# An RWKV-7 / HGRN2 mixer on one core: the RWKV state scan on half tiles of TensorE, one projection moved, and new planner figures

## The chip, the core and the metric

The kernel runs on one NeuronCore of a Trainium2 chip. The metric is the device time of one execution in microseconds (us). Before the change its median over 3 runs is 1031.55 us (1031.42 to 1031.56). TensorE is called PE below (PEld is its weight load, which overlaps the products), VectorE DVE, ScalarE ACT, GpSimd POOL, SyncE SP.

## The reference, cut to what matters

One layer over 512 frames of width 2048, in float32. One input projection feeds two mixers: 16 RWKV-7 heads of 64 columns, and 8 HGRN2 heads of 128. The gated outputs are concatenated, projected back, added to the residual and normalised. The part that the change rewrites is the recurrence of an RWKV head over its 64x64 state S:

```python
def step(S, inp):
    r_t, w_t, k_t, v_t, a_t, b_t = inp
    sa = jnp.einsum('bhij,bhj->bhi', S, a_t)
    S = S * w_t[:, :, None, :] + sa[..., None] * b_t[:, :, None, :] + v_t[..., None] * k_t[:, :, None, :]
    return S, jnp.einsum('bhij,bhj->bhi', S, r_t)
```

The kernel evaluates it in 8 chunks of 64 frames. Within a chunk, 64x64 score matrices and one triangular inverse stand for the recurrence; only the 64x64 state goes from chunk to chunk, one step of the scan for each.

## The kernel before, in words

**The bulk.** Both projections are dense products with 128x128 stationary tiles and 512 moving columns. Each float32 operand is split into a high and a low part (`xh`, `xl`; `wh`, `wl`), and `three` (L485) issues three products for each pair of tiles. This takes 3948 products of that kind on PE, those of the small preparations in the same number format included. The weights come in by DMA into `wr`, ACT makes `wh` and DVE `wl`.

**The rest** is recorded by small helpers, so that its instructions have the helpers' lines: `mm` (L348) for float32 products, `act` (L361, L362) on ACT, `tt` (L371), `stt` (L380), `copy` (L413) on DVE. A float32 product is two instructions in the profile. Heads are treated in pairs (`p` = 0 to 7), and pairs in groups of two (`grp` = 0 to 3), so four heads at a time. For a group there are, in this order: scores (`rwkv_prep`, 64-row stationary tiles), the inversion (`rwkv_invert`, 32x32 tiles), `folded` (64x64 tiles), `rwkv_scan`, and `outputs` (128-row tiles of 64 columns).

**The scan before.** The states of the two heads of a pair lie as the two 64x64 blocks on the diagonal of a 128x128 tile `bd`, whose other blocks are zero. A step of the scan has two bursts on PE. The first (called the state burst below) multiplies the stationary `ar` with the old state: two products of 128x128x128, one for each pair, into `mix` banks. DVE subtracts the upper half from `zz`, ACT scales the old state into the other `bd`, and ACT or DVE copies the lower half into the output tile. The second (the update burst) multiplies `bk` with `zz`, again two whole products, and DVE adds the diagonal blocks to the state, with four `stt` of 64x64. There are 7 steps with a state burst and 7 with an update burst in each group, 56 bursts in all.

**What sets the order.** All instructions are put in order when the program is built. `Plan` holds a clock for each engine and adds a cost figure for every operation. It lets the dense products run through, and takes the next operation of a thread (a generator for a head, a group, an eviction) when its operands should be there by the figures. PE's products are of three modes: `main` (the dense ones), `whole` (float32, full tiles) and `narrow` (a stationary tile of fewer than 128 rows or columns). `TURNS` holds a figure for each change of mode (0.1 into narrow, 0.11 out of it). After a narrow burst no other begins for 1.5 by the plan's clock (`REST`), and a burst that is ready is held back for a moment so that another may join it (`HOLD`). `_order` lists the projections, one for each name and number: k, r, v, z, q, f, g and i.

Of the kernel before, what the change touches and what calls it, by code (L numbers as in the profile page):

```python
# [7 lines left out]
F32 = mybir.dt.float32  # L8
# [30 lines left out]
def _order():  # L39

    o = [("w", 0)]
    for g in range(NPAIR // 2):
        for p in (2 * g, 2 * g + 1):
            o += [("k", p), ("r", p), ("v", p)]
            if g:
                o.append(("z", p - 2))
        o += [("q", 2 * g), ("f", 2 * g), ("q", 2 * g + 1), ("f", 2 * g + 1)]
        if g % 2 == 0:
            o.append(("i", g // 2))
        o += [("g", 2 * g), ("g", 2 * g + 1)]  # L50
    return o + [("z", NPAIR - 2), ("z", NPAIR - 1)]


# [3 lines left out]
    return o + [(2, 14), (2, 15), (3, 13), (3, 14), (3, 15)]  # L57


SETS = {AF.Sigmoid: ("sigmoid",), AF.Tanh: ("exp", "sigmoid"), AF.Exp: ("exp", "ln"), AF.Ln: ("ln",)}  # L60


class Plan:
# [194 lines left out]
def mixer_kernel(ctx, tc, head, x_r, w_all, par, up, ln_wb, consts, hmask, out):  # L258
# [25 lines left out]
    def take(tag, shape=(P, T), dt=F32):  # L284

        if not plan.free(tag):
            raise RuntimeError(f"no room: {tag}")
        slot = min(plan.slots[tag])
        plan.slots[tag].remove(slot)
        if tag in PBUFS:  # L290
            t = ppool.tile(list(shape), dt, tag=tag, name=nm(tag), bufs=PBUFS[tag])
            plan.banks.add(t.tensor.name)
        else:
            t = st(tag, list(shape), dt)
        name = t.tensor.name
        plan.busy[name] = (slot[1], None)
        tags[name] = tag
        return t

    def drop(*tiles):  # L300
        for t in tiles:
            name = t.tensor.name
            plan.slots[tags.pop(name)].append((plan.used.get(name, plan.count), plan.busy[name][0]))
# [27 lines left out]
    def size(ap):  # L331
        n = 1
        for s in ap.shape[1:]:
            n *= s
        return n

    def mm(o, l, r, start=True, stop=True, cost=None, **kw):
        m, n = size(l), size(r)
        narrow = m < P or l.shape[0] < P
        if cost:  # L340
            pass
        elif r.dtype == F32R:
            cost = n / 2400 + 0.0145
        elif narrow:
            cost = 0.0135 + n * 0.0002 if m <= 32 else 0.06 if m <= 64 else 0.115
        else:
            cost = n / 600 + 0.005
        return Op([("pe", cost, lambda: pe.matmul(o, l, r, start=start, stop=stop, **kw))], [l, r], [o],  # L348
                  mode="narrow" if narrow else "main" if r.dtype == F32R else "whole")
# [4 lines left out]
    def moved(o, i):  # L354

        return 0.1 if o.shape[0] < P else 0.0

    def act_way(o, i, f, scale=1.0, bias=0.0):
        cost = 0.09 + size(o) * 0.00085 + moved(o, i) + (0.06 if isinstance(scale, bass.AP) else 0.0)
        if f == AF.Copy:  # L360
            return "act", cost, lambda: sc_e.activation(o, i, f, scale=scale)  # L361
        return "act", cost, lambda: sc_e.activation(o, i, f, scale=scale, bias=bias)  # L362
# [4 lines left out]
    def dve_op(reads, o, f, n=None, per=0.00104, base=0.07):  # L367
        return Op([("dve", base + (n or size(o)) * per, f)], reads, [o])

    def tt(o, a, b, f=ALU.mult):  # L370
        return dve_op([a, b], o, lambda: dve.tensor_tensor(o, a, b, f),  # L371
                      base=0.16 if o.shape[0] < P and size(o) == C and o.tensor.name in tags else 0.07)

    def ts(o, a, s1, s2, f1, f2=None):
        if f2 is None:
            return dve_op([a], o, lambda: dve.tensor_scalar(o, a, s1, None, f1), per=0.0008)
        return dve_op([a], o, lambda: dve.tensor_scalar(o, a, s1, s2, f1, f2), per=0.0008)

    def stt(o, a, s, b, f1, f2):
        return dve_op([a, b], o, lambda: dve.scalar_tensor_tensor(o, a, s, b, f1, f2), per=0.00113,  # L380
                      base=0.085 if o.shape[0] == P else 0.25 if size(o) == C else 0.165)

    def red(o, i):
        return dve_op([i], o, lambda: dve.tensor_reduce(o, i, AX.X, ALU.add), size(i))
# [2 lines left out]
        return dve_op([i], o, lambda: dve.copy_predicated(o, m, i))  # L387

    def dtr(o, i):
        return dve_op([i], o, lambda: dve.transpose(o, i), per=0.0019)  # L390

    def dve_tt_way(o, a, b, f=ALU.mult):
# [12 lines left out]
    def memset(o, v):  # L405
        return Op([("pool", 0.1 + size(o) * 0.00083, lambda: pool.memset(o, v))], [], [o])

    def copy(o, i, scale=1.0):

        if scale != 1.0:  # L410
            f = lambda: dve.tensor_scalar(o, i, scale, None, ALU.mult)
        else:
            f = lambda: dve.tensor_copy(o, i)  # L413
        return Op([act_way(o, i, AF.Copy, scale), ("dve", 0.075 + size(o) * 0.00105 + moved(o, i), f)], [i], [o])

    def blocks(t, n):

# [2 lines left out]
    def turned(dst, src, tmp, rows=4):  # L420

        far = dpool.tile([P, rows, size(tmp) // rows], F32, tag=nm("far"), name=nm("far"))
        yield dtr(tmp.rearrange("p b c j -> p c b j"), src)
        yield lambda: by_now(tmp)
        yield lambda: plan.clock["sp"] <= plan.clock["pe"] + 0.2
        send(far, tmp.rearrange("p b c j -> p b (c j)"))
        there = plan.busy[tmp.tensor.name] = (plan.clock["sp"] + 4.0, "dma")
        for b in range(rows):
            yield lambda: there[0] <= plan.clock["pe"] and plan.clock["sp"] <= plan.clock["pe"] + 0.2
            send(dst(b).rearrange("i a c j -> i a (c j)"), far[:, b].rearrange("(a i) x -> i a x", a=4))  # L430
        plan.ready[dst(0).tensor.name] = (plan.clock["sp"] + 4.0, "dma")

# [236 lines left out]
    def head_sums(f, g, hl):  # L669

        own = slice(0, 64)
        yield tt(f[own], f[own], g[own], ALU.add)
        yield act(hl[own], f[own], AF.Copy)
        yield tt(hl[64:128], f[own], hl[own].bitcast(F32), ALU.subtract)

    def rwkv_prep(S, p):
        if p == 0:
# [227 lines left out]
    def rwkv_scan(SS, sc):  # L905

        pcs, ars, bks, zzs, os = ([S[n] for S in SS] for n in ("pc", "ar", "bk", "zz", "o"))  # L910
        yield room(bd=4)
        bdss = [[take("bd", [P, P]) for _ in range(2)] for _ in SS]

        def block(ps, h):
            return ps[hc[h], h * 64 : h * 64 + 64]

        for bds, o in zip(bdss, os):
            for t in bds:
                yield memset(t, 0.0)
            yield memset(o[0:64, 0], 0.0)  # L920
        olds = [None] * 2
        for c in range(NCH):
            more = c < NCH - 1
            zs = [zz[:, :, c] for zz in zzs]
            news = [bds[c % 2] for bds in bdss]
            pxs = []
            if c > 0:
                yield landed(*olds)
                yield room(mix=2)
                for ar, old in zip(ars, olds):  # L930
                    pxs.append(take("mix"))
                    yield mm(pxs[-1][:, :P], ar[:, c], old)
                for px, z in zip(pxs, zs):
                    yield tt(z[0:64], z[0:64], px[0:64, :P].rearrange("p (a j) -> p a j", j=32), ALU.subtract)
                if more:
                    for new, old, pc in zip(news, olds, pcs):
                        yield act(new, old, AF.Copy, scale=pc[:, c : c + 1])
                for px, o in zip(pxs, os):
                    yield copy(o[64 * (c % 2) : 64 * (c % 2) + 64, c // 2], px[64:128, :P])
                    drop(px)  # L940
            if more:
                yield landed(*zzs)
                yield room(mix=2)
                pds = [take("mix") for _ in SS]
                for pd, bk, z in zip(pds, bks, zs):
                    yield mm(pd[:, :P], bk[:, c], z)
                for pd, new, pc in zip(pds, news, pcs):
                    for h in range(2):
                        yield stt(new[hc[h], hc[h]], block(pd, h), pc[hc[h], c : c + 1],
                                  new[hc[h], hc[h]], ALU.mult, ALU.add)  # L950
                    drop(pd)
                olds = news
        drop(*ars, *bks, *pcs, *bdss[0], *bdss[1])

# [795 lines left out]
```

## Time and profile before

| | |
|---|---|
| median of 3 runs | 1031.55 us |
| the profiled execution's own time | 1033.02 us |
| its span, from the first to the last instruction | 1031.2 us |
| what lies around the span | 1.8 us |
| PE, DVE, ACT, POOL busy | 1020.1, 789.9, 478.4, 42.6 us |
| mean granted clock of TensorE | 1.000 |

The profiled execution took 1.47 us longer than the median. "Busy" counts each instruction from its start to its end, so that products that overlap in the array count as one stretch. A row of the groups or of a tile reads: line, engine, operation, written tile<-read tiles, stationary rows*columns, (partitions)x(moving columns), count | busy us, mean ns | idle time before. A row of the timeline reads: start us, us, engine, line, operation, tiles, count of merged instructions.

### The profile page before, as it was taken

Reading aid. Unit: us, or ns where it says so; the run is one execution under the profiler, and the core shown is the slowest. Engines: PE = TensorE matmul, PEld = TensorE weight load, DVE = VectorE, ACT = ScalarE, POOL = GpSimd, SP = SyncE. Lnnn points to the kernel's source line nnn. Section 1 sums busy time; section 2 is a strip of 40 time slices with the busy share of each in tenths; the row PEclk is TensorE's granted clock in tenths of the full one; section 3 lists DMA queues with packets and bytes.
Section 4 is the critical chain, followed back from the end, with each engine's and each line's share of the span. In section 5 each row is a group of like instructions: output and inputs, shape, how many; then the busy total and the mean of one; then the engine's idle time right before and its main releaser. Section 6 shows DMA issues by size and latency. Waiting matters only on the chain.

```text
span 1031.2 us, 19527 instructions
## 1 busy us (share of the span) xinstructions
PE 1020.1 (99%) x7636; PEld 843.2 (82%) x7636; DVE 789.9 (77%) x1687; ACT 478.4 (46%) x898; POOL 42.6 (4%) x77
## 2 busy tenths in 40 slices
PE   9999999999999999999999999999999999999997
PEld 8888878888878888888887888887888888888885
DVE  7477997679779988698998758887998888526556
ACT  6457344545363356464534554636435544323321
POOL 0000001001000010020000100100001010000000
PEclk9999999999999999999999999999999999999999
DMA  9134442233635322345353243253432256435613
GB/s 337 53 104 127 138 125 88 78 103 113 183 105 157 122 73 81 92 138 183 105 152 105 82 114 118 92 172 111 147 106 81 63 175 226 149 117 172 200 55 133
DMA packets 58700, 130.82 MB, mean 127 GB/s; under 512 B 9840, under 2 KB 25712, under 8 KB 58480
## 3 DMA queue, kind: packets, MB, share of 16 engines
q1 hardware_dynamic: 58464, 129.37, 39.7%
q8 instruction: 60, 0.98, 0.4%
q14 instruction: 32, 0.26, 0.1%
q10 hardware_dynamic: 144, 0.20, 0.1%
HBM read 111.06 MB, written 18.48 MB: 126 GB/s over the span
## 4 chain that ended last, share of the span: by engine, by line
PE 94%; DMA 2%; DVE 2%; ACT 1%; issue 1%; SPq 0%; DVEq 0%; ACTq 0%
PE main L485 71%; PE mix L348 9%; PE mix L485 8%; PE main L1275 3%; PE main L348 2%; DMA q<-far 1%; DMA far<-q 1%; PE mix L1225 0%; DVE inv L380 0%; SPq L327 0%; DVE wl L371 0%; DVE big L371 0%; DVE q L413 0%; DVE big L390 0%; ACT wh L361 0%
## 5 line engine op out<-in xcount | busy, mean ns | idle before, releaser
L485 PE MATMUL main<-xh,wl 128*128 128x512 f32 x864 | 340.0, 393 | 0.0
L485 PE MATMUL main<-xh,wh 128*128 128x512 f32 x864 | 339.5, 393 | 0.0
L485 PE MATMUL main<-xl,wh 128*128 128x512 f32 x864 | 339.0, 392 | 0.0
L361 ACT ACTIVATE wh<-wr 128x512 fp32r<-128x512 f32 x299 | 185.7, 626 | 194.4 <-PE main L485 139.0
L371 DVE TENSOR_TENSOR wl<-wr,wh 128x512 fp32r<-128x512 f32 x299 | 203.6, 682 | 56.0 <-ACT wh L361 53.9
L485 PEld LDWEIGHTS main<-xh,wh 128*128 128x128 f32 x864 | 162.4, 188 | 33.1
L485 PEld LDWEIGHTS main<-xh,wl 128*128 128x128 f32 x864 | 162.3, 188 | 33.1
L485 PEld LDWEIGHTS main<-xl,wh 128*128 128x128 f32 x864 | 162.3, 188 | 33.0
L485 PE MATMUL main<-wh,xl 128*128 128x512 f32 (+1 forms) x262 | 102.4, 391 | 0.0
L485 PE MATMUL main<-wh,xh 128*128 128x512 f32 (+1 forms) x262 | 101.8, 389 | 0.5 <-ACT t L362 0.5
L485 PE MATMUL main<-wl,xh 128*128 128x512 f32 (+1 forms) x262 | 101.9, 389 | 0.0
L485 PEld LDWEIGHTS main<-wh,xh 128*128 128x128 f32 x262 | 49.2, 188 | 10.8 <-ACT t L362 1.0
L485 PEld LDWEIGHTS main<-wh,xl 128*128 128x128 f32 x262 | 49.2, 188 | 10.0
L485 PEld LDWEIGHTS main<-wl,xh 128*128 128x128 f32 x262 | 49.2, 188 | 9.9
L362 ACT ACTIVATE t<-main,om 128x512 f32<-128x512 f32 x33 | 22.3, 686 | 51.9 <-PE main L485 42.6
L380 DVE SCALAR_TENSOR_TENSOR bd<-mix,pc,bd 64x64 f32<-64x64 f32 x112 | 31.7, 283 | 11.6 <-PE mix L348 7.8
L371 DVE TENSOR_TENSOR inv<-inv,inv 64x30 f32<-64x30 f32 (+14 forms) x120 | 38.5, 321 | 2.7
L371 DVE TENSOR_TENSOR inv<-inv 64x30 f32<-64x30 f32 (+14 forms) x120 | 38.5, 321 | 2.5
L380 DVE SCALAR_TENSOR_TENSOR t<-main,pr,t 128x511 f32<-128x511 f32 x33 | 24.3, 745 | 19.6 <-ACT t L362 19.5
L361 ACT ACTIVATE t<-mix 64x128 f32<-64x128 f32 (+2 forms) x66 | 18.0, 276 | 44.3 <-DVE zz L371 23.5
L371 DVE TENSOR_TENSOR t<-t,tot 128x256 f32<-128x256 f32 x96 | 37.2, 418 | 0.2
L362 ACT ACTIVATE t<-main 128x512 f32<-128x512 f32 x32 | 18.6, 593 | 28.7 <-PE main L485 28.6
(228 smaller groups left out, 1408.1 us busy)
## 6 DMA issues: line engine op xcount, KB each, us to landing
wr<-w_all SPq DMA_DIRECT2D x156, 512.0 KB, 3.6
q<-head SPq DMA_DIRECT2D x15, 448.0 KB, 5.8
far<-ksq SPq DMA_DIRECT2D x22, 256.0 KB, 3.2
far<-q SPq DMA_DIRECT2D x8, 512.0 KB, 5.0
q<-far SPq DMA_DIRECT2D x32, 128.0 KB, 4.4
g<-x_r SPq DMA_DIRECT2D x16, 256.0 KB, 4.0
t<-far SPq DMA_DIRECT2D x56, 64.0 KB, 3.5
spill<-g SPq DMA_DIRECT2D x12, 256.0 KB, 2.8
```

Of the source, the lines that this page charges most:

```text
L348: return Op([("pe", cost, lambda: pe.matmul(o, l, r, start=start, stop=stop, **kw))], [l, r], [o], mode="narrow" if narrow else "main" if ...
L361: return "act", cost, lambda: sc_e.activation(o, i, f, scale=scale)
L362: return "act", cost, lambda: sc_e.activation(o, i, f, scale=scale, bias=bias)
L371: return dve_op([a, b], o, lambda: dve.tensor_tensor(o, a, b, f), base=0.16 if o.shape[0] < P and size(o) == C and o.tensor.name in tags e ...
L380: return dve_op([a, b], o, lambda: dve.scalar_tensor_tensor(o, a, s, b, f1, f2), per=0.00113, base=0.085 if o.shape[0] == P else 0.25 if s ...
L485: pe.matmul(ps, l, r, start=first and i == 0, stop=last and i == 2)
L1275: pe.matmul(pss[a], *ops, start=k == 0 and low == of == 0, stop=k == KT - 1 and low == 1)
```

## The change

1. The states of a pair's two heads are stacked in one tile `bd` of 128 rows and 64 columns (the first head in rows 0 to 63, the second in rows 64 to 127). The state burst becomes four products with 64 stationary rows and 128 columns, 64 moving columns each; the two heads of a pair go to two banks and lie on the two row halves of the array. The update burst becomes four products with 128 stationary rows and 64 columns, 64 moving columns; the two heads go to the two column halves, all in one bank. In the planner they are narrow, at 0.07 and 0.063 a product.
2. Round them: four subtractions and four copies of 64x64 where there were two each of 64x128; two `stt` of 128x64 in place of four of 64x64; the scaled copy is 128x64; half of the clearing of `bd` is left out.
3. `_order`: in the groups 0 and 2 the first of the two g projections (an HGRN gate) stands ahead of the i projection.
4. Figures of the planner: DVE costs that depend on where the operand lies (`banked`), other bases for `stt` and the DVE transpose, a landing time that grows with the size (`late`), and Exp without the `ln` table. The argument 0.15 in `head_sums` has no effect there, since the condition behind it in `tt` does not hold for a tile of 512 columns. None of these figures adds or removes an instruction.

```diff
-        if g % 2 == 0:
-            o.append(("i", g // 2))
-        o += [("g", 2 * g), ("g", 2 * g + 1)]
+        o.append(("g", 2 * g))
+        if g % 2 == 0:
+            o.append(("i", g // 2))
+        o.append(("g", 2 * g + 1))
...
-SETS = {AF.Sigmoid: ("sigmoid",), AF.Tanh: ("exp", "sigmoid"), AF.Exp: ("exp", "ln"), AF.Ln: ("ln",)}
+SETS = {AF.Sigmoid: ("sigmoid",), AF.Tanh: ("exp", "sigmoid"), AF.Exp: ("exp",), AF.Ln: ("ln",)}
...
+    def banked(ap):
+
+        return 0.00104 if ap.tensor.name in plan.banks else 0.00076
...
-                      base=0.085 if o.shape[0] == P else 0.25 if size(o) == C else 0.165)
+                      base=0.085 if o.shape[0] == P and size(o) > P else 0.12 if o.shape[0] == P
+                      else 0.21 if size(o) == C else 0.165)
...
+        late = 4.2 + max(0, size(tmp) - T) * 0.002
+        there = plan.busy[tmp.tensor.name] = (plan.clock["sp"] + late, "dma")
...
-        bdss = [[take("bd", [P, P]) for _ in range(2)] for _ in SS]
+        bdss = [[take("bd", [P, C]) for _ in range(2)] for _ in SS]
...
-                for ar, old in zip(ars, olds):
-                    pxs.append(take("mix"))
-                    yield mm(pxs[-1][:, :P], ar[:, c], old)
-                for px, z in zip(pxs, zs):
-                    yield tt(z[0:64], z[0:64], px[0:64, :P].rearrange("p (a j) -> p a j", j=32), ALU.subtract)
+                pxs = [take("mix") for h in range(2)]
+                for i, (ar, old) in enumerate(zip(ars, olds)):
+                    for h in range(2):
+                        yield mm(pxs[h][:, i * C : i * C + C], ar[hc[h], c], old[hc[h]], cost=0.07)
+                for i, z in enumerate(zzs):
+                    for h in range(2):
+                        zh = z[0:64, hb[h], c]
+                        yield tt(zh, zh, pxs[h][0:64, i * C : i * C + C].rearrange("p (a j) -> p a j", j=32),
+                                 ALU.subtract)
...
-                pds = [take("mix") for _ in SS]
-                for pd, bk, z in zip(pds, bks, zs):
-                    yield mm(pd[:, :P], bk[:, c], z)
-                for pd, new, pc in zip(pds, news, pcs):
-                    for h in range(2):
-                        yield stt(new[hc[h], hc[h]], block(pd, h), pc[hc[h], c : c + 1],
-                                  new[hc[h], hc[h]], ALU.mult, ALU.add)
-                    drop(pd)
+                pd = take("mix")
+                for i, (bk, z) in enumerate(zip(bks, zzs)):
+                    for h in range(2):
+                        yield mm(pd[hc[h], i * C : i * C + C], bk[:, c, hc[h]], z[:, hb[h], c], cost=0.063)
+                for i, (new, pc) in enumerate(zip(news, pcs)):
+                    yield stt(new, pd[:, i * C : i * C + C], pc[:, c : c + 1], new, ALU.mult, ALU.add)
+                drop(pd)
```

The first place in the order is PE at a state burst of the first group, before. `main` with `xh` and `xl` is the dense stream; `bd` is the state, `q` holds `ar`, `mix` is a bank.

```order
L485 MATMUL main_2182<-xh_70,wh_2128 128x512
L485 MATMUL main_2182<-xl_86,wh_2128 128x512
L348 MATMUL mix_2198<-bd_2144,q_449 128x128
L348 MATMUL mix_2207<-bd_2146,q_756 128x128
L485 MATMUL main_2182<-xh_70,wl_2129 128x512
L485 MATMUL main_2182<-xh_71,wh_2128 128x512
```

And a state burst of the same group in the changed program.

```order
L494 MATMUL main_2319<-xh_78,wh_2341 128x512
L494 MATMUL main_2319<-xl_94,wh_2341 128x512
L349 MATMUL mix_2425<-bd_2232,q_449 128x64
L349 MATMUL mix_2426<-bd_2232,q_449 128x64
L349 MATMUL mix_2425<-bd_2234,q_769 128x64
L349 MATMUL mix_2426<-bd_2234,q_769 128x64
L494 MATMUL main_2319<-xh_78,wl_2342 128x512
L494 MATMUL main_2319<-xh_79,wh_2341 128x512
```

Two products became four, and they still stand alone between dense products. Of the 28 state bursts of the program, 21 stand alone like this in the changed order, 6 next to whole products and one next to narrow ones; of the 28 update bursts 22 stand alone, 3 next to whole and 3 next to narrow products.

The second place is PE at the outputs of the first group, before (`zz` and `big` are the inputs of `outputs`).

```order
L485 MATMUL main_2506<-xh_83,wl_2559 128x512
L348 MATMUL mix_2620<-zz_1080,big_713 64x64 x16
L348 MATMUL mix_2621<-zz_1377,big_713 64x64 x16
L485 MATMUL main_2680<-xh_68,wh_2585 128x512
L485 MATMUL main_2680<-xl_84,wh_2585 128x512
```

And the same place in the changed program, where `q` with `q` are the scores of a later pair.

```order
L494 MATMUL main_2748<-xh_73,wh_2733 128x512
L349 MATMUL mix_2779<-zz_1044,big_719 64x64 x16
L349 MATMUL mix_2780<-zz_1351,big_719 64x64 x16
L349 MATMUL main_2825<-q_2323,q_2324 128x128
L349 MATMUL main_2826<-q_2323,q_2324 128x128
L349 MATMUL main_2825<-q_2323,q_2324 128x128
```

A narrow burst of scores has joined the outputs here, and again in the third group; 32x32 products of the inversion join 48-column ones twice instead of once. In all, PE has 102 bursts between dense products before and 100 after. The last group's outputs stand behind 3156 dense products before and behind 3189 after.

The third place is DVE in a step of the first group's scan, before (`wl` is the dense stream's share of DVE).

```order
L371 TENSOR_TENSOR zz_1080<-zz_1080,mix_2255 64x4x32
L371 TENSOR_TENSOR zz_1377<-zz_1377,mix_2265 64x4x32
L413 COPY t_951<-mix_2265 64x128
L380 SCALAR_TENSOR_TENSOR bd_2144<-mix_2280,pc_646,bd_2144 64x64 x2
L380 SCALAR_TENSOR_TENSOR bd_2146<-mix_2281,pc_903,bd_2146 64x64
L371 TENSOR_TENSOR wl_2296<-wr_2174,wh_2295 128x512
L380 SCALAR_TENSOR_TENSOR bd_2146<-mix_2281,pc_903,bd_2146 64x64
```

And in the changed program.

```order
L372 TENSOR_TENSOR zz_1044<-zz_1044,mix_2425 64x2x32
L372 TENSOR_TENSOR zz_1044<-zz_1044,mix_2426 64x2x32
L372 TENSOR_TENSOR zz_1351<-zz_1351,mix_2425 64x2x32
L372 TENSOR_TENSOR zz_1351<-zz_1351,mix_2426 64x2x32
L397 STREAM_TRANSPOSE ksq_2430<-t_967 128x4x4x32
L372 TENSOR_TENSOR wl_2470<-wr_2288,wh_2469 128x512
L385 SCALAR_TENSOR_TENSOR bd_2233<-mix_2467,pc_667,bd_2233 128x64
```

Four subtractions stand where two stood, and one `stt` for each pair where two stood. Over the program the counts on DVE go from 112 to 56 for the `stt` on `bd`, from 56 to 112 for the subtractions, and from 28 to 45 for the copies of `mix` into the output tile; on ACT those copies go from 28 to 67. The number of dense products (3948) is the same.

More of the change, by code (lines that the diff above doesn't have):

```diff
@@ L368, in dve_op, with tt @@
         return Op([("dve", base + (n or size(o)) * per, f)], reads, [o])
-    def tt(o, a, b, f=ALU.mult):
+    def tt(o, a, b, f=ALU.mult, base=None):
         return dve_op([a, b], o, lambda: dve.tensor_tensor(o, a, b, f),
-                      base=0.16 if o.shape[0] < P and size(o) == C and o.tensor.name in tags else 0.07)
+                      base=base or 0.16 if o.shape[0] < P and size(o) == C and o.tensor.name in tags else 0.07)
+    def banked(ap):
+        return 0.00104 if ap.tensor.name in plan.banks else 0.00076
     def ts(o, a, s1, s2, f1, f2=None):
         if f2 is None:
-            return dve_op([a], o, lambda: dve.tensor_scalar(o, a, s1, None, f1), per=0.0008)
-        return dve_op([a], o, lambda: dve.tensor_scalar(o, a, s1, s2, f1, f2), per=0.0008)
+            return dve_op([a], o, lambda: dve.tensor_scalar(o, a, s1, None, f1), per=banked(a))
+        return dve_op([a], o, lambda: dve.tensor_scalar(o, a, s1, s2, f1, f2), per=banked(a))
     def stt(o, a, s, b, f1, f2):
         return dve_op([a, b], o, lambda: dve.scalar_tensor_tensor(o, a, s, b, f1, f2), per=0.00113,
-                      base=0.085 if o.shape[0] == P else 0.25 if size(o) == C else 0.165)
+                      base=0.085 if o.shape[0] == P and size(o) > P else 0.12 if o.shape[0] == P
+                      else 0.21 if size(o) == C else 0.165)
     def red(o, i):
@@ L389, in dtr @@
     def dtr(o, i):
+        if i.shape[0] == P:
+            return dve_op([i], o, lambda: dve.transpose(o, i), per=0.0011, base=0.05)
         return dve_op([i], o, lambda: dve.transpose(o, i), per=0.0019)
@@ L413, in copy @@
             f = lambda: dve.tensor_copy(o, i)
-        return Op([act_way(o, i, AF.Copy, scale), ("dve", 0.075 + size(o) * 0.00105 + moved(o, i), f)], [i], [o])
+        return Op([act_way(o, i, AF.Copy, scale), ("dve", 0.07 + size(o) * banked(i) + moved(o, i), f)], [i], [o])
     def blocks(t, n):
@@ L426, in turned @@
         send(far, tmp.rearrange("p b c j -> p b (c j)"))
-        there = plan.busy[tmp.tensor.name] = (plan.clock["sp"] + 4.0, "dma")
+        late = 4.2 + max(0, size(tmp) - T) * 0.002
+        there = plan.busy[tmp.tensor.name] = (plan.clock["sp"] + late, "dma")
         for b in range(rows):
@@ L430, in turned @@
             send(dst(b).rearrange("i a c j -> i a (c j)"), far[:, b].rearrange("(a i) x -> i a x", a=4))
-        plan.ready[dst(0).tensor.name] = (plan.clock["sp"] + 4.0, "dma")
+        plan.ready[dst(0).tensor.name] = (plan.clock["sp"] + late, "dma")
     splits = plan.queue()
@@ L673, in head_sums @@
         yield act(hl[own], f[own], AF.Copy)
-        yield tt(hl[64:128], f[own], hl[own].bitcast(F32), ALU.subtract)
+        yield tt(hl[64:128], f[own], hl[own].bitcast(F32), ALU.subtract, 0.15)
     def rwkv_prep(S, p):
@@ L911, in rwkv_scan @@
         yield room(bd=4)
-        bdss = [[take("bd", [P, P]) for _ in range(2)] for _ in SS]
-        def block(ps, h):
-            return ps[hc[h], h * 64 : h * 64 + 64]
+        bdss = [[take("bd", [P, C]) for _ in range(2)] for _ in SS]
         for bds, o in zip(bdss, os):
-            for t in bds:
-                yield memset(t, 0.0)
+            yield memset(bds[0], 0.0)
             yield memset(o[0:64, 0], 0.0)
@@ L923, in rwkv_scan @@
             more = c < NCH - 1
-            zs = [zz[:, :, c] for zz in zzs]
             news = [bds[c % 2] for bds in bdss]
-            pxs = []
             if c > 0:
-                yield landed(*olds)
+                yield landed(*olds, n=4)
                 yield room(mix=2)
-                for ar, old in zip(ars, olds):
-                    pxs.append(take("mix"))
-                    yield mm(pxs[-1][:, :P], ar[:, c], old)
-                for px, z in zip(pxs, zs):
-                    yield tt(z[0:64], z[0:64], px[0:64, :P].rearrange("p (a j) -> p a j", j=32), ALU.subtract)
+                pxs = [take("mix") for h in range(2)]
[7 more added lines that the diff above has]
+                                 ALU.subtract)
                 if more:
@@ L937, in rwkv_scan @@
                         yield act(new, old, AF.Copy, scale=pc[:, c : c + 1])
-                for px, o in zip(pxs, os):
-                    yield copy(o[64 * (c % 2) : 64 * (c % 2) + 64, c // 2], px[64:128, :P])
-                    drop(px)
+                for i, o in enumerate(os):
+                    for h in range(2):
+                        yield copy(o[64 * (c % 2) : 64 * (c % 2) + 64, c // 2, hc[h]], pxs[h][64:128, i * C : i * C + C])
+                drop(*pxs)
             if more:
-                yield landed(*zzs)
-                yield room(mix=2)
-                pds = [take("mix") for _ in SS]
-                for pd, bk, z in zip(pds, bks, zs):
-                    yield mm(pd[:, :P], bk[:, c], z)
-                for pd, new, pc in zip(pds, news, pcs):
+                yield landed(*zzs, n=4)
+                yield room(mix=1)
+                pd = take("mix")
+                for i, (bk, z) in enumerate(zip(bks, zzs)):
                     for h in range(2):
-                        yield stt(new[hc[h], hc[h]], block(pd, h), pc[hc[h], c : c + 1],
-                                  new[hc[h], hc[h]], ALU.mult, ALU.add)
-                    drop(pd)
+                        yield mm(pd[hc[h], i * C : i * C + C], bk[:, c, hc[h]], z[:, hb[h], c], cost=0.063)
+                for i, (new, pc) in enumerate(zip(news, pcs)):
+                    yield stt(new, pd[:, i * C : i * C + C], pc[:, c : c + 1], new, ALU.mult, ALU.add)
+                drop(pd)
                 olds = news
```

## The prediction

> **What bounds the kernel now.** I read the page first, then the waits of PE, then the chain of waits, and last the timeline around single bursts.
>
> ```profile
> PE 1020.1 (99%) x7636; PEld 843.2 (82%) x7636; DVE 789.9 (77%) x1687; ACT 478.4 (46%) x898; POOL 42.6 (4%) x77
> PEclk9999999999999999999999999999999999999999
> ```
>
> PE is busy for 1020.1 of 1031.2 us, at the full granted clock in all 40 slices. DVE is next with 77%.
>
> ```profile
> PE mix L348 <- DVE ksq L371: 2.2, 2, 1.5
> PE mix L348 <- ACT ksq L1492: 1.5, 1, 1.5
> PE mix L1225 <- DVE inv L1223: 1.1, 1, 1.1
> PE mix L348 <- ACT wh L361: 0.8, 1, 0.8
> PE main L485 <- ACT t L362: 0.5, 1, 0.5
> ```
>
> All that PE waited for others is 6.1 us. The 1.1 lies at the start and the 1.5 in the normalisation at the end, and the change touches neither. So 2.2 + 0.8 + 0.5 = 3.5 us in the body is the most that other engines could give back. What PE itself does therefore decides, start to start, and the chain of waits shows the pace of the dense stream:
>
> ```profile
> 749.10 28.58 PE main L485 x126
> ```
>
> 28.58 / 126 = 0.227 us for each dense product. I price a burst by what it takes out of this stream: from the start of the last dense product before it to the start of the second one after it, less 2 x 0.227 = 0.454.
>
> **The change part by part.** The old state burst in the timeline (start, us):
>
> ```profile
> 201.05 0.39 PE L485 MATMUL main<-xl,wh 128*128 128x512 f32 x1
> 201.28 0.60 PE L348 MATMUL mix<-bd,q 128*128 128x128 f32 x4
> 201.64 0.48 PE L485 MATMUL main<-xh,wl 128*128 128x512 f32 x1
> 201.95 0.40 PE L485 MATMUL main<-xh,wh 128*128 128x512 f32 x1
> ```
>
> 201.95 - 201.05 - 0.454 = 0.45 us. The first instruction starts 0.23 after the dense one, the ordinary pace, so entering costs nothing. The update burst has the same form:
>
> ```profile
> L348 PE MATMUL mix<-bd,q 128*128 128x128 f32 x112 | 17.2, 275 | 0.0
> L348 PE MATMUL mix<-zz,q 128*128 128x128 f32 x112 | 17.2, 275 | 0.0
> ```
>
> Both are 112 instructions, four in a burst, so 28 bursts of each kind; 56 x 0.45 = 25 us is what the scan takes from PE now.
>
> The trace has no burst of four small products. It has long ones of the same tiles. First the outputs, 128 rows and 64 columns, 64 moving, the form of the new update burst:
>
> ```profile
> 243.66 0.40 PE L485 MATMUL main<-xh,wl 128*128 128x512 f32 x1
> 243.99 2.08 PE L348 MATMUL mix<-zz,big 128*64 128x64 f32 x64
> 246.00 0.50 PE L485 MATMUL main<-xh,wh 128*128 128x512 f32 x1
> 246.34 0.40 PE L485 MATMUL main<-xl,wh 128*128 128x512 f32 x1
> ```
>
> The price is 246.34 - 243.66 - 0.454 = 2.23 us for 32 products. One instruction lasts 0.22, so the 64 starts take 2.08 - 0.22 = 1.86, or 0.058 a product. 32 x 0.058 = 1.87, and 0.36 is left that doesn't go with the number. It can be seen at the ends: the burst begins 0.33 after the dense product (0.10 more than the pace), and the second dense product comes 0.34 after the first (0.11 more); the rest is the unoverlapped start and end of the burst. Four products then cost 0.36 + 4 x 0.058 = 0.59, against 0.45: **+0.14 an update burst**.
>
> The scores have the state burst's new tile, 64 rows and 128 columns, but 128 moving columns:
>
> ```profile
> 70.44 0.39 PE L485 MATMUL main<-xl,wh 128*128 128x512 f32 x1
> 70.76 1.16 PE L348 MATMUL main<-q,q 64*128 64x128 f32 x16
> 71.75 1.06 PE L348 MATMUL mix<-q,q 64*128 64x128 f32 x16
> 72.74 0.50 PE L485 MATMUL main<-xh,wl 128*128 128x512 f32 x1
> 73.08 0.39 PE L485 MATMUL main<-xh,wh 128*128 128x512 f32 x1
> ```
>
> 73.08 - 70.44 - 0.454 = 2.19 us for 16 products. The second half paces 8 products in about 0.9, so 0.112 each, and 2.19 - 16 x 0.112 = 0.40 is fixed. What would the pace be with 64 moving columns? If the moving columns set it, 0.058, as in the outputs. If the loading of the weights sets it, it stays at 0.11, since the stationary tile still has 128 columns. The loads say which:
>
> ```profile
> L348 PEld LDWEIGHTS mix<-q,q 64*128 64x128 f32 x144 | 8.7, 188 | 0.4 <-issue 0.4
> L348 PEld LDWEIGHTS mix<-zz,big 128*64 128x64 f32 x256 | 7.8, 138 | 1.4 <-issue 1.1 <-ACT t L361 0.4
> L348 PEld LDWEIGHTS mix<-t 128*32 128x32 f32 x640 | 7.5, 110 | 3.8 <-issue 3.6
> 70.75 0.30 PEld L348 LDWEIGHTS main<-q,q 64*128 64x128 f32 x4 [0.35 <-issue]
> ```
>
> A load lasts 188, 138 and 110 ns for 128, 64 and 32 columns, so some 0.8 ns a column on a fixed part: an estimate of about 0.10 us for 128. The last row shows it at the entrance of the scores, where nothing is in the way yet: four loads, two for each row half, end 0.30 after the first starts, and one lasts 0.19, so the second two began 0.11 after the first two. That a short stream doesn't hurry the loads is seen where streams are shorter than loads:
>
> ```profile
> 802.03 0.70 PE L348 MATMUL mix<-t,t 128*32 128x16 f32 x62
> 802.66 0.71 PE L348 MATMUL mix<-zz,q 128*128 128x128 f32 x4
> 803.13 0.48 PE L485 MATMUL main<-xh,wl 128*128 128x512 f32 x1
> ```
>
> 62 starts in 0.70 - 0.18 = 0.52 us, 8.5 ns each, so 34 ns for four instructions, one on each column quarter. Sixteen moving columns would take 14 ns by the 0.112 of a product of 128 in the scores; 32 columns of weights take some 27. The loads set the pace. I therefore take 0.11 for the new state burst: 0.40 + 4 x 0.11 - 0.05 (its last stream is half as long) = 0.79, **+0.34 a state burst**. The other end, with the stream's pace, is 0.40 + 4 x 0.058 - 0.05 = 0.58, so +0.13.
>
> On this point the Trainium skill (TensorE: Matmul & The Clock Gate, section LDWEIGHTS) states that a load takes the number of columns divided by 1.2, in ns, whatever the number of rows, which is 107 ns for 128 columns; by it the state burst costs the upper of the two values. No run shows a 64-row load of 128 columns with so short a stream.
>
> Neighbours. Beside whole products the step from one to the other costs what it does beside dense ones, by the bursts' ends above, so 27 state bursts cost +0.34, and the one beside narrow products some +0.1: 9.3 us. 25 update bursts cost +0.14: 3.5 us. Three stand next to narrow products of another tile size. Before, a whole burst in that place took 803.13 - 802.66 = 0.47; now it needs 4 x 0.058, and some 0.2 for the change of tile: about -0.05 each, -0.15 us. In three other places two narrow bursts now share one entrance and exit; that saves 0.36 less the same 0.2, about 0.5 us in all. PE's sum is 9.3 + 3.5 - 0.15 - 0.5 = **+12.1 us**. With the stream's pace it is 27 x 0.21 = 5.7 less: +6.4.
>
> DVE and ACT.
>
> ```profile
> L380 DVE SCALAR_TENSOR_TENSOR bd<-mix,pc,bd 64x64 f32<-64x64 f32 x112 | 31.7, 283 | 11.6 <-PE mix L348 7.8 <-ACT wh L361 1.5
> L371 DVE TENSOR_TENSOR zz<-zz,mix 64x128 f32<-64x128 f32 x56 | 13.9, 277 | 11.9 <-PE mix L348 11.8
> L361 ACT ACTIVATE t<-mix 64x128 f32<-64x128 f32 x42 | 11.3, 273 | 24.0 <-DVE zz L371 23.5 <-DVE t L413 0.2
> ```
>
> Half of the `stt` go, 56 x 0.28 = 16 us less; the subtractions double in number at half the size, between nothing and 14 us more; there are 56 more copies at up to 0.27, about 15 us shared by both engines. Together that is within 15 us of nothing for DVE, and some us more for ACT, which has half its time free. All of it is hidden behind the dense stream: before, only 2.2 + 0.8 + 0.5 us of it got through to PE. If the cover were gone, two more subtractions at 0.28 in each of 28 steps would be late: 15 us. It holds, as most bursts stand many dense products apart. The halved clearing on POOL, the moved projection (the same dense products, 48 of them exchanged in order) and the figures of the planner cost nothing by themselves; they decide where the 3.5 us of waits fall, and I know no row that tells which go. Since PE is up to 12 us later than the plan thinks at the joins, I take 1.5 of the 3.5 off.
>
> **Sum.** The profiled execution took 1033.02 us, its span 1031.2; 1033.02 + 12.1 - 1.5 = 1043.6, and as the median lies 1.47 below that execution, 1042.1 us. I say 1042.0.
>
> **The rivals.**
>
> (a) The moving columns set the pace of the state burst. Then 1031.55 + 6.4 - 1.5 = 1036.5. The scores can't exclude it, since their loads and streams are equally long; the row with 16 columns speaks against it.
>
> (b) A new wait near the end. The last group's outputs move 33 dense products later, 7.5 us. Before, the last gated tile was made and split for the output projection like this:
>
> ```profile
> 872.07 0.74 DVE L380 SCALAR_TENSOR_TENSOR g<-g,half,t 128x512 f32<-128x512 f32 x1
> 882.53 0.62 ACT L361 ACTIVATE xh<-g 128x512 fp32r<-128x512 f32 x1
> ```
>
> 9.7 us lay between, so about 2 are left. If the transposes through DRAM in between land over 2 us later than before, PE waits for the rest, 2 to 4 us: 1044 to 1046. The last group's longer bursts speak for it, the planner's landing times, now longer, against.
>
> (c) Faster. The small tiles work side by side, so four products would take the array half of what two whole ones take, and the entrances and exits would overlap with the dense stream in bursts this short: 56 x 0.22 = 12.5 us less, 1019. It decides from the point where the fixed 0.36 to 0.40 falls under 0.22. The Trainium skill (TensorEngine Tiling (Array Packing), section Theoretical Speedup) promises up to twofold for a small dimension of at most 64. Against it stands that both long bursts begin 0.32 to 0.33 after the dense product and are followed by a step of 0.34, ends which a short burst has too.
>
> (d) Nothing to measure: (a) together with all 3.5 us of waits gone is 1031.55 + 2.9 = 1034.5, still slower, so no change needs a smaller fixed part than any burst shows.
>
> **How the numbers follow.** Main case 0.62, (a) 0.18, (b) 0.10, (c) 0.06, (d) 0.04. The main case is 1040 to 1044.5 by the waits (all gone or all kept: 1040.2 to 1043.7, and 1 us for the neighbours). The range takes in (a) and (b): 1036 to 1046.5; outside lie (c), (d) and a tail. About 0.2% (2 us) is what a measurement of this kernel can tell from no change. Faster by more 0.06, within it 0.04, slower 0.90.
>
> **What would show it.** In the changed trace a lone state burst, priced as above from the dense product before it to the second one after it, should come to 0.79, with its pairs of weight loads 0.11 apart, and a lone update burst to 0.59. PE busy should stay at 99% and the `stt` on `bd` be 56. The forecast is wrong if the loads of the state burst come 0.06 apart, if a burst of four starts less than 0.3 after the dense product, or if waits in PE's list exceed 5 us in the body.

## The result, and the profile after

The changed kernel takes 1042.99 us (median of 5 runs, 1042.25 to 1044.65), and the kernel before 1031.56 us beside it (median of 5). The ratio is 1.0114 (95% interval 1.0102 to 1.0127), so it is slower by 11.4 us, and 1 us from the forecast. The profiled execution of the changed kernel is the one of 1042.99 us. First the head of its page.

```profile
span 1041.1 us, 19987 instructions
PE 1031.6 (99%) x7860; PEld 838.8 (81%) x7860; DVE 773.9 (74%) x1724; ACT 470.9 (45%) x917; POOL 37.0 (4%) x69
PEclk9999999999999999999999999999999999999999
```

The span is 9.9 us longer, and PE is as full as before (99%), at full clock. DVE has 16.0 us less to do and ACT 7.5 us less, and nothing of that reached the end: neither is what the kernel waits for. All waits of PE (us in total, times, the longest one):

```profile
PE mix L349 <- ACT ksq L1498: 1.5, 1, 1.5
PE mix L1231 <- DVE inv L1229: 1.1, 1, 1.1
PE main L494 <- DVE wl L372: 0.9, 2, 0.6
PE main L494 <- DVE xl L372: 0.7, 1, 0.7
PE main L1281 <- ACT xh L362: 0.4, 1, 0.4
```

Without the first two, which the kernel before has too, 2.0 us are left of 3.5. None of the old three is among them, and three new ones are. From here on "the waits" are those in this list without the 1.5 and the 1.1. The list counts a wait only from the end of the last product on (0.39 us after its start, where the next dense one would start after 0.227), so that by PE's starts each of them costs some 0.2 to 0.3 us more.

Next the state burst in PE's timeline, and its weight loads:

```profile
225.50 0.39 PE L494 MATMUL main<-xl,wh 128*128 128x512 f32 x1
225.81 0.66 PE L349 MATMUL mix<-bd,q 64*128 64x64 f32 x8
226.41 0.50 PE L494 MATMUL main<-xh,wl 128*128 128x512 f32 x1
226.75 0.39 PE L494 MATMUL main<-xh,wh 128*128 128x512 f32 x1
```

```profile
225.81 0.52 PEld L349 LDWEIGHTS mix<-bd,q 64*128 64x128 f32 x8 [0.35 <-issue]
```

The price is 226.75 - 225.50 - 0.454 = 0.80 us. The burst begins 0.31 after the dense product, its eight instructions take 0.60 up to the next dense one, and a step of 0.34 follows. The eight loads, two side by side, take 0.52; with 0.19 for the last pair, as before, three steps lie in 0.33, which is 0.11 each. The update burst:

```profile
207.10 0.39 PE L494 MATMUL main<-xl,wh 128*128 128x512 f32 x1
207.42 0.45 PE L349 MATMUL mix<-zz,q 128*64 128x64 f32 x8
207.80 0.50 PE L494 MATMUL main<-xh,wl 128*128 128x512 f32 x1
208.14 0.39 PE L494 MATMUL main<-xh,wh 128*128 128x512 f32 x1
```

208.14 - 207.10 - 0.454 = 0.59 us. The groups show what became of the work round the bursts:

```profile
L385 DVE SCALAR_TENSOR_TENSOR bd<-mix,pc,bd 128x64 f32<-128x64 f32 x56 | 13.5, 279 | 17.6 <-PE mix L349 17.4
L372 DVE TENSOR_TENSOR zz<-zz,mix 64x64 f32<-64x64 f32 x112 | 18.0, 207 | 25.9 <-PE mix L349 25.9
L362 ACT ACTIVATE t<-mix 64x64 f32<-64x64 f32 x67 | 11.0, 216 | 26.7 <-DVE zz L372 26.1
```

The `stt` went from 31.7 to 13.5 us, the subtractions from 13.9 to 18.0. ACT's copies in the scan went from 28 of 64x128 to 67 of 64x64.

To see where the 9.9 us lie I summed PE's steps from start to start over the whole trace, by what starts and what went before, less 0.227 for each dense product. Scan bursts: 22.3 us before and 33.3 after (+11.0); the longer steps of dense products behind bursts: +0.6; other bursts: -0.2; steps too long for any product, the waits: -1.5. That is +9.9.

Of the 2.0 us of new waits, 1.3 lie in the output projection, round 887 us (0.3 more follow at 979 us, and the 0.4 lies at 8 us, ahead of the dense stream). DVE and PE there, from the timeline:

```profile
885.38 1.14 DVE L385 SCALAR_TENSOR_TENSOR g<-t,half,t 128x128 f32<-128x128 f32 x4 [4.84 <-DMA t<-far]
886.44 0.68 DVE L372 TENSOR_TENSOR wl<-wr,wh 128x512 fp32r<-128x512 f32 x1
887.64 0.68 DVE L372 TENSOR_TENSOR xl<-g,xh 128x512 fp32r<-128x512 f32 x1
```

```profile
886.16 0.39 PE L494 MATMUL main<-wh,xh 128*128 128x512 f32 x1
887.18 0.50 PE L494 MATMUL main<-wl,xh 128*128 128x512 f32 x1 [0.63 <-DVE wl L372]
888.38 0.50 PE L494 MATMUL main<-wh,xl 128*128 128x512 f32 x1 [0.70 <-DVE xl L372]
```

The gating of a last-group tile (`g<-t,half,t`) stands in DVE's queue and waits 4.84 us for a tile that comes back from DRAM (`t<-far`). The `wl` of the dense stream and a split `xl` are queued behind it, and PE waits 0.63 and 0.70 us for them. By PE's starts the two waits cost 888.38 - 886.16 - 0.454 = 1.77 us.

### The profile page after: what moved, and what is told of

Same layout as the page of the kernel before. It is cut to its first block, busy times and chain, and to the rows that moved or that the text cites. A ratio compares the mean times of both kernels' runs of the same rounds, so it can differ in the third digit from the quotient of the medians.

```text
span 1041.1 us, 19987 instructions
## 1 busy us (share of the span) xinstructions
PE 1031.6 (99%) x7860; PEld 838.8 (81%) x7860; DVE 773.9 (74%) x1724; ACT 470.9 (45%) x917; POOL 37.0 (4%) x69
## 4 chain that ended last, share of the span: by engine, by line
PE 93%; DMA 3%; DVE 2%; issue 0%; ACT 0%; SPq 0%; DVEq 0%
PE main L494 71%; PE mix L349 10%; PE mix L494 8%; PE main L1281 3%; DMA wr<-w_all 2%; PE main L349 1%; DMA t<-far 1%; DMA q<-head 1%; DVE wl L372 1%; DVE inv L385 0%; DVE t L372 0%; SPq L328 0%; ACT t L362 0%; PE mix L353 0%; DVE q L385 0%
## 5 line engine op out<-in xcount | busy, mean ns | idle before, releaser
L362 ACT ACTIVATE t<-mix 64x64 f32<-64x64 f32 (+4 forms) x106 | 21.7, 238 | 49.3 <-DVE zz L372 26.1
L372 DVE TENSOR_TENSOR zz<-zz,mix 64x64 f32<-64x64 f32 x112 | 18.0, 207 | 25.9 <-PE mix L349 25.9
```

## The experiments

Theory: the tile form of the scan's products costs what the long bursts of before say (a fixed 0.36 to 0.40 us and a pace, which in the state burst is the loads'), and the planner part moves waits only. Rivals: the moving columns set the pace; the order and the figures carry a part of the result of their own. Before was timed again beside each batch: 1031.65 and 1031.18 us.

**1. The changed kernel with the old scan.**

```diff
-                        yield mm(pxs[h][:, i * C : i * C + C], ar[hc[h], c], old[hc[h]], cost=0.07)
+                    yield mm(pxs[-1][:, :P], ar[:, c], old)
...
-                        yield mm(pd[hc[h], i * C : i * C + C], bk[:, c, hc[h]], z[:, hb[h], c], cost=0.063)
+                    yield mm(pd[:, :P], bk[:, c], z)
```

(and the subtractions, copies and `stt` of before with them)

> The changed kernel with the scan of before (two whole products in a burst); the moved projection and all new figures stay. Theory 1 (the small products cost PE about 12 us, the rest of the change only moves PE's waits): 1043.0 - 12.1 = 1031, within 1029.5 to 1032.5, so level with the kernel before or up to 2 us faster, and each burst again at 0.45 us. Rival (the order and the figures cost a good part of the 11.4 us, by later outputs and waits at the output projection): 1034 or more.

Measured 1027.60 us (1027.27 to 1027.75 in 5 runs), ratio to before 0.9959 (0.9946 to 0.9971), 15.4 us faster than the changed kernel and 1.9 us under the range that was expected. Its waits:

```profile
PE mix L349 <- ACT ksq L1501: 1.5, 1, 1.5
PE mix L1234 <- DVE inv L1232: 1.1, 1, 1.1
PE main L1284 <- ACT xh L362: 0.4, 1, 0.4
```

Only 0.4 is left. So the tile form does the harm, and the rest of the change gives 4 us. Against the kernel before, its span is 5.7 us shorter (the profiled execution of before lay 1.47 us above its median, so the medians are only 4 us apart); PE's steps give 4.6 of that to waits (3.1 by the list, which counts less of each), 0.8 to the scan bursts and 0.6 to the steps behind bursts, with 0.3 against it. Against the changed kernel its span is 15.6 us shorter: some 11.7 of that lie in the scan bursts, 3.0 in waits and 1.2 in the steps behind bursts. The waits at the output projection are gone too, so it is the new form of the scan that makes them. This is the version to keep; it beats both kernels.

**2. The kernel before with the new scan alone** (the reverse of the edit above, in the kernel before).

> The kernel before with the new scan alone; order and figures of before. Theory 1: 56 bursts at +0.34 and +0.14 us less some joined entrances, 1031.6 + 11 to 13 = 1042.5 to 1044.5. Rival (order and figures carry part of the loss): under 1040.

Measured 1052.89 us, ratio 1.0201 (1.0186 to 1.0217): 8 us above the upper end of what was expected. The scan bursts take 33.3 us by PE's steps, the same as in the changed kernel. The rest is waits, 9.2 us of them, of which the largest:

```profile
PE mix L348 <- DVE ksq L371: 3.7, 5, 1.0
PE main L348 <- issue: 3.0, 1, 3.0
PE main L485 <- DVE xl L371: 1.0, 1, 1.0
```

So the same bursts under the old figures and order give a worse plan, 10 us worse than with the new ones. My bound of 3.5 us on the planner part did not allow for that. Some 4.6 of the 10 us are the one wait of 3.0 on "issue", for which no engine is named, and 1.6 lost behind it (both are taken up in the last section).

**3. The figures alone** (the old scan, the old order of projections, the new figures).

```diff
-        o.append(("g", 2 * g))
         if g % 2 == 0:
             o.append(("i", g // 2))
-        o.append(("g", 2 * g + 1))
+        o += [("g", 2 * g), ("g", 2 * g + 1)]
```

(on the kernel of experiment 1)

> The kernel before with the new planner figures alone: old scan, old place of the projection. The version with figures and moved projection ran at 1027.6, 4 us under the kernel before. If the figures take PE's waits away: 1027 to 1029, with under 1 us of waits in the body. Rival (the moved projection does it): 1031 to 1033.

Measured 1028.98 us, ratio 0.9972 (0.996 to 0.9984), as expected, with 0.7 us of waits:

```profile
PE mix L348 <- issue: 0.5, 1, 0.5
PE mix L348 <- DVE ksq L371: 0.2, 1, 0.2
```

The figures alone give most of the 4 us.

**4. The moved projection alone** (the kernel before with the new lines of `_order`).

> The kernel before with the moved projection alone: old scan, old figures. If the figures do it: 1031 to 1033, with waits for the square sums of the heads as before. Rival (the moved projection does it): 1027 to 1029.

Measured 1039.28 us, ratio 1.0069 (1.005 to 1.0087). Both expectations fall: it is slower by 8 us, with 7.9 us of waits:

```profile
PE main L486 <- DVE t L381: 2.6, 1, 2.6
PE mix L349 <- DVE ksq L372: 1.9, 3, 1.0
PE main L486 <- DVE wl L372: 1.2, 1, 1.2
```

With the new figures the same move takes 1.4 us off (1028.98 to 1027.60). Why the old figures let the move run into just these waits was not tried.

**5. Twice the moving columns in the state burst** (the states in tiles of 128 columns, the second 64 zero and never read).

```diff
-                        yield mm(pxs[h][:, i * C : i * C + C], ar[hc[h], c], old[hc[h]], cost=0.07)
+                        yield mm(pxs[h][:, i * P : i * P + P], ar[hc[h], c], old[hc[h]], cost=0.07)
```

> The changed kernel with 128 moving columns in the state burst in place of 64; the second 64 are zeros whose products nobody reads. PE's order is that of the changed kernel. Theory 1 (loads pace it): four loads in a row take as long as before and only the last stream is 0.05 longer: 28 x 0.05 = 1.5 us more, 1044.5. Rival (the moving columns pace it): each of four products 0.05 more, 28 x 0.21 = 6 us more: 1049.

Measured 1044.05 us, ratio 1.0119 (1.0105 to 1.0133), 1.1 above the changed kernel and 0.5 from what was expected. A state burst:

```profile
224.40 0.39 PE L494 MATMUL main<-xl,wh 128*128 128x512 f32 x1
224.72 0.71 PE L349 MATMUL mix<-bd,q 64*128 64x128 f32 x8
...
225.70 0.39 PE L494 MATMUL main<-xh,wh 128*128 128x512 f32 x1
```

225.70 - 224.40 - 0.454 = 0.85. Twice the stream costs 0.05 a burst, which is the one longer last stream that the prediction took off. The loads set the pace.

**6. The state burst in squares.** Eight products of 64x64 stand for four of 64x128, so that each load has 64 columns and four fit side by side. First as single operations of the planner (with the burst's size in `landed` set to 8):

```diff
-                        yield mm(pxs[h][:, i * C : i * C + C], ar[hc[h], c], old[hc[h]], cost=0.07)
+                        for e in range(2):
+                            yield mm(pxs[h][hc[e], i * C : i * C + C], ar[hc[h], c, hc[e]], old[hc[h]], cost=0.035)
```

> The changed kernel with the state burst as eight products of 64x64 stationary tiles in place of four of 64x128; all else the same, the result too. Theory 1 (loads pace the state burst, so half the columns on twice as many tiles take half the time): the eight products pace as in the folded part, 4 x 0.06 us, a burst costs about 0.60 in place of 0.79, 28 x 0.19 = 5.3 us less: 1037.7. Rival (each product of a row half costs a fixed 0.11, whatever its columns): eight products cost 0.9 or, two by two, 0.45, so 1043 or more.

Measured 1051.78 us, ratio 1.0194 (1.018 to 1.0208), 14 above what was expected. The bursts were as short as expected (0.60), but the planner made another order of it, with 95 bursts where 100 stood, and the last HGRN heads came to stand alone at the end of the projection:

```profile
845.08 1.06 PE L349 MATMUL mix<-t 128*32 128x16 f32 x64 [5.63 <-ACT t L362]
...
854.54 1.09 PE L349 MATMUL mix<-t 128*32 128x32 f32 x32 [4.49 <-ACT t L362]
```

13.7 us of waits in all. Between and behind them, from 845 to 860 us, the granted clock stood at 0.50, which is a part of the rest of the loss. So this run says nothing against the squares themselves. Then with the order kept: two squares are issued as one planned operation.

```diff
+    def several(cost, *products):
+        def issue():
+            for o, l, r in products:
+                pe.matmul(o, l, r, start=True, stop=True)
...
+                        yield several(0.07, *((pxs[h][hc[e], i * C : i * C + C], ar[hc[h], c, hc[e]], old[hc[h]])
+                                              for e in range(2)))
```

> As the experiment with square tiles, eight products of 64x64 in the state burst, but issued two by two where the changed kernel issues one, so that PE's order and the plan are those of the changed kernel. Theory 1 (a state burst now costs 0.59 in place of 0.79, and the 15 us that the first try lost lay in waits of another order): 28 x 0.20 = 5.6 us less than the changed kernel, 1043.0 - 5.6 = 1037.4. Rival (the square tiles themselves lose time somewhere that the price of a burst doesn't show): 1043 or more.

Measured 1035.31 us, ratio 1.0036 (1.0023 to 1.0049), 2.1 under what was expected. A burst:

```profile
224.33 0.39 PE L494 MATMUL main<-xl,wh 128*128 128x512 f32 x1
224.65 0.46 PE L917 MATMUL mix<-bd,q 64*64 64x64 f32 x16
225.04 0.50 PE L494 MATMUL main<-xh,wl 128*128 128x512 f32 x1
225.38 0.39 PE L494 MATMUL main<-xh,wh 128*128 128x512 f32 x1
```

225.38 - 224.33 - 0.454 = 0.60, 0.20 less than with 128 columns, for the same products: 28 x 0.20 = 5.6 us, and 1.2 us of waits fewer (0.8 for 2.0). That makes 6.8 of the 7.7 us between it and the changed kernel; by PE's starts the waits fell by 2.2 us, which closes the sum. The entrance (0.32) and the step behind (0.34) stay, and with them it is slower than the whole products.

**7. Each product of the update burst twice**, the order kept.

```diff
+                        yield several(0.063, *[(pd[hc[h], i * C : i * C + C], bk[:, c, hc[h]], z[:, hb[h], c])] * 2)
```

> The changed kernel with each product of the update burst issued twice in a row; PE's order otherwise kept, the result too. Theory 1 (0.36 of the 0.59 is paid once a burst, at its ends, and a product costs 0.058): two equal tiles in a row can't run side by side with each other as the alternating ones do, so between 4 x 0.058 and 8 x 0.058 more a burst, 28 x 0.23 = 6.5 us to 13 us: 1049.5 to 1056. Rival (short products hide behind the ends, and the price is for the burst, not the product): under 1045.

Measured 1049.18 us, ratio 1.0166 (1.015 to 1.0183), 6.2 above the changed kernel, with 1.6 us of waits. A burst:

```profile
206.64 0.39 PE L494 MATMUL main<-xl,wh 128*128 128x512 f32 x1
206.96 0.73 PE L917 MATMUL mix<-zz,q 128*64 128x64 f32 x16
...
207.96 0.39 PE L494 MATMUL main<-xh,wh 128*128 128x512 f32 x1
```

207.96 - 206.64 - 0.454 = 0.87: four more products cost 0.28, or 0.07 each, and four cost 0.59 altogether. So 0.59 - 0.28 = 0.31 of the burst doesn't go with the number of products. The doubled products stand twice in a row on the same half of the array, where those of the long burst alternate, so 0.31 may be low; with the 0.058 of the long burst it is 0.36. At 28 bursts, 0.28 makes 7.8 us; the total rose by 6.2, just under the range that was expected, as by PE's starts the waits fell by some 1.3.

Put together (medians, us; "rest" is the median less the waits):

| scan | planner | time | waits | rest |
|---|---|---|---|---|
| whole | old figures, old order | 1031.55 | 3.5 | 1028.1 |
| whole | old figures, new order | 1039.28 | 7.9 | 1031.4 |
| whole | new figures, old order | 1028.98 | 0.7 | 1028.3 |
| whole | new figures, new order | 1027.60 | 0.4 | 1027.2 |
| half tiles | old figures, old order | 1052.89 | 9.2 | 1043.7 |
| half tiles | new figures, new order | 1042.99 | 2.0 | 1041.0 |
| squares in the state burst | new figures, new order | 1035.31 | 0.8 | 1034.5 |

The tile form is seen in the rest (some 14 to 16 us between whole products and half tiles), the planner mostly in the waits. The rest is good to some 2 us: the waits come from one execution, while the times are medians, and the list counts less than a wait costs. Where there are many waits (the second and the fifth row) the rest takes up some of what they cost.

## Why the prediction was right, and where it was not

**The bound and the prices held.** PE is the bound in both kernels. The state burst was priced at 0.79 and takes 0.80, the update burst at 0.59 and takes 0.59; the pairs of loads stand 0.11 apart. PE's sum was +12.1 us; the scan bursts and the steps behind them made +11.6. Its term for a change of tile, some 0.2 us, had no row beside it; where a scan burst stands next to products of another tile, the starts at the change lie 0.11 to 0.20 us apart in the changed trace.

**Rival (a) fell.** Experiment 5 doubles the stream for 0.05 us a burst, and experiment 6 halves the loads' columns and takes 0.20 off. The Trainium skill (TensorE: Matmul & The Clock Gate, section LDWEIGHTS) gives a load the number of columns divided by 1.2, in ns, so 107 for 128 columns, and the 0.11 between pairs agrees, now with a stream that is too short to hide it. With (a) fell (d), which needed it.

**Rival (c) fell** by the ends of the short bursts: 0.31 to 0.32 at the entrance where the pace is 0.227, 0.34 behind. Experiment 7 gives 0.31 us or more of 0.59 that doesn't go with the products, above the 0.22 from which (c) would have decided. The Trainium skill (TensorEngine Tiling (Array Packing), section Key Properties) says that a change of the tiling mode drains TensorE. The rows agree with a cost at both ends; that a drain is its cause no run here shows.

**Rival (b) came in, at its lower end.** The last group's outputs came late for the output projection, as the rival had it. PE lost 1.3 us there by the list and 1.77 by its starts, where the rival had 2 to 4. It waited not for the last gated tile itself but for what was queued behind its `stt` on DVE. With the old scan (experiment 1) nothing waits there. The total stayed near the forecast because the old waits went at the same time.

**The step on waits had the right size for the wrong reason.** The prediction took 1.5 of 3.5 us off and said that the planner part "cost nothing by themselves". The net is -1.5. But it is made of all 3.5 us gone and 2.0 us of new waits, and the parts alone are larger: the moved projection alone +7.7, the figures alone -2.6, both together -4.0 with the old scan, and -9.9 with the new one (1052.89 to 1042.99). What failed is the bound. As the most that a better order can give back, 3.5 us was a bit low (experiment 1 got 4.6 us by PE's starts, on which the four old waits cost 4.2), and it says nothing about what a worse order can add. That the forecast came within 1 us is in part luck: under the new figures and order the tile form costs 15.4 us (1042.99 - 1027.60), 3 more than PE's sum, mostly in waits, and the planner part gives 4.0 back where 1.5 was taken off.

**DVE and ACT.** DVE lost 16.0 us, 1 more than the 15 that I allowed; ACT lost 7.5 where I said some more. Neither mattered to the end.

**Open** are the place of the old figures' waits with the moved projection, what makes the ends of a burst of small tiles cost what they do, and, short of a run that tests it, the wait of 3.0 us on "issue" in experiment 2.

## What to carry to other kernels

Where TensorE is full of dense products, a short burst of half tiles was priced here by its two ends first (some 0.3 to 0.4 us) and by the number of stationary columns per load next. Packing pays only when a burst has enough products to carry its ends. An estimate from the prices of this case: two products of 128x64 cost 2 x 0.058 where the whole product that they replace costs some 0.22 (half of the old burst's 0.45), so a burst needs some seven of them (0.36 / (0.11 - 0.058)) to get even; two of 64x128 cost 2 x 0.11, as much as the whole one, and never get even. A long burst of the same tile, split into a fixed part and a pace, gives that price before anything is built. Waits seen in a trace tell roughly what a better order can give back, never what another order can cost: a planner's figures, its order of work and the work's sizes are to be tried together, and two forms of a product compared with the order kept.

## What the runs showed of the hardware

The wait of 3.0 us in experiment 2, from 604.4 to 607.4 us, was most likely one for TensorE's own instructions. The trace has 61 loads of 16 KB on the queue that its page calls "q8 instruction", one for some 260 of the 15,800 recorded instructions of PE and PEld. One began at 603.98 us, just before PE stopped, and took 2.17 us, the longest of the 61 (median 1.0). It landed 1.3 us before PE went on; DVE, ACT and POOL were idle meanwhile. The four shorter waits on "issue" in experiments 3, 4 and 6 (0.2 to 0.7 us) end in the same way, 1.4 to 1.5 us behind such a load, and each follows a run of small products. No run changed the loads, so this is not shown.

Behind that wait, TensorE's dense products ran at about half pace and then came back. First two products in the slow stretch, then two behind it:

```profile
610.10 0.63 PE L485 MATMUL main<-xh,wh 128*128 128x512 f32 x1
610.52 0.63 PE L485 MATMUL main<-xl,wh 128*128 128x512 f32 x1
...
613.03 0.40 PE L485 MATMUL main<-xh,wl 128*128 128x512 f32 x1
613.26 0.39 PE L485 MATMUL main<-xh,wh 128*128 128x512 f32 x1
```

The step was 0.42 where it is 0.23 otherwise. Seven steps were so, at 0.427 each, and one on either side at 0.33: 1.6 us on top of the wait, which is part of the 2.7 us by which this kernel's rest stands above the changed kernel's. The granted clock was 0.53 in this stretch (608.9 to 612.5 us) and 1.00 on either side.

A `stt` of 128x64 took 279 ns and one of 64x64 took 283: twice the rows cost DVE nothing, so stacking the two heads halved its time in the state update.
